# A hybrid attention and RG-LRU block on one core: V's scratch laid out dense by head pair, and the shares' spreads put into the scores' banks

## The chip, the cores and the metric

The kernel runs on one NeuronCore of a Trainium2 chip. The metric is the device time of one execution in microseconds (us), the median of several runs. One further execution is profiled; its own time stands beside its span below. The engines are called PE (TensorE's matmuls), PEld (its weight loads, which run ahead of the matmuls), DVE (VectorE), ACT (ScalarE), POOL (GpSimd) and SP (SyncE, which here only issues transfers).

## The reference, cut to what matters

One decoder block over 2048 positions of width 1024, batch 1, in float32:

```python
proj = x @ W_in + b_in                      # 1024 -> 9216 columns: q, k, v, gates, LRU input
for g, (window, dilation) in enumerate(((128, 1), (512, 4), (2048, 16))):
    # 8 heads of 64; keys t - j*dilation; blocks of 128 queries against 256 keys
    o[g], lse[g] = dilated_band_attention(rope(q[g]), rope(k[g]), v[g], window, dilation)
attn = sum(softmax(lse over g)[g] * o[g])   # the shares of the three groups, per head and position
y_a = (attn * silu(g_attn)) @ w_attn_proj
y_b = (rg_lru(conv(u)) * silu(g_lru)) @ w_lru_proj
out = (sigmoid(gA) * y_a + sigmoid(gB) * y_b) @ w_out + b_out
x = layer_norm(2 ** 0.25 * x + out)
```

A "share" in this text is a softmax weight of a group, one number for each head and position.

## The kernel before

Large products are made of three float32r products each (a tile is split into a high part and a rest, and high by high, high by rest and rest by high are summed in PSUM), which is why almost all matmuls have the form 128x128 by 128x512.

**First stage** (from the start to about 1452 us). The input projection, by a planner: `where` lists 36 pairs of column blocks for each of two halves of the sequence, and `product` (L633) issues 12 matmuls a tick. Results go through chains (generators) that DVE, ACT and POOL serve by a budget per tick. `v_chain` is the one for V: a 128x512 piece of V, channels on the partitions, is turned by four transposes on PE, ACT copies it out of PSUM into one of two tiles `vs` (L374), and SP sends it to the scratch `v_scr` in DRAM (L378). There are 48 such pieces: 3 groups, 4 head pairs, 4 chunks of 512 positions. ACT waits for the transfer that last left a `vs` tile before it fills it again.

**Attention stage** (about 1452 to 1785 us). Its order is written out by hand in the loop `for G in range(NG + 1)`: 48 groups, four of them to a unit, 12 units. A unit is one head pair of one dilation group; it has 16 blocks of 128 queries, and a group takes four of them. On PE a group holds, in this order: `turn_p` of a pair of blocks of the group before (transposes of the probabilities, L1003, into the PSUM banks `t0` and `t1`, one buffer each, copied out by ACT at L1016 and by DVE or ACT for the second half), two `scores` (L975) with another `turn_p` behind them, `values` (L1035, bank `o`, copied out by DVE at L1051), and then twelve matmuls of the other branch's projection (`yb_part`, L1205) in four parts. The scores lie in the banks `s0` and `s1`, two buffers each, one bank for each head of the pair; DVE adds the mask and takes the row minimum (L987), ACT takes the exponential (L989). These eight banks (`s0` and `s1` twice, `t0`, `t1`, `o`, `y`) are all of PSUM.

When the three units of a head pair are done, the shares are worked out (`weights`) and written to DRAM, and come back as `wh`. A **spread** then multiplies them by a selector matrix (L1129, one matmul 128x128 by 128x512), so that each share stands on all 64 partitions of its head, and DVE multiplies the group's output by the bank it lands in (L236, `o<-o,w`). There are 48 spreads: 4 head pairs, 4 chunks, 3 groups. 36 of them run inside the attention loop, up to two in a group, G = 19 to 25, 31 to 37 and 43 to 48: the first between the second and third part of the yb matmuls, the second between the third and fourth. The other 12 run in the next stage out of the bank `z`. Two groups, G = 20 and G = 37, have spreads but no yb matmuls (`rests`), since the next chunk's inputs are then loaded. Every fourth group also ends with a transpose of the minima and sums (`turn_ml`, L1056, bank `o`).

V comes back from `v_scr` unit by unit: `v_parts` issues four transfers of 256 KB for the next unit. At the start of the stage SP issues, one behind the other, V of unit 0, q and k of unit 1, the weights `wlr` and the other branch's inputs `hx` (L1176), V of unit 1 and the second half of `hx`. POOL splits each `hx` into its two parts (L1180, L1181) for the yb matmuls.

**Last stages.** The rest of yb with the last 12 spreads (to about 1873 us), then y_a, the output product and the layer norm. When the attention loop ends, its pool of PSUM is closed and another opened over the same eight banks (`fp`: four buffers of `y`, three of `z`).

Of the kernel before, what the change touches and what calls it, by code (L numbers as in the profile page):

```python
# [8 lines left out]
F32 = mybir.dt.float32  # L9
F32R = mybir.dt.float32r  # L10
AF = mybir.ActivationFunctionType
# [4 lines left out]
P = 128  # L16
S = 2048
# [3 lines left out]
CH = 512  # L21
HP = 4
# [9 lines left out]
def hybrid_block_kernel(ctx: ExitStack, tc: tile.TileContext, a: dict, out: bass.AP):  # L32
    nc = tc.nc
    sp, act, dve, pool, pe = nc.sync, nc.scalar, nc.vector, nc.gpsimd, nc.tensor

    def flat(t):
        return t.bitcast(F32)


    dram = ctx.enter_context(tc.tile_pool(name="dram", bufs=1, space=DRAM))  # L40
# [6 lines left out]
    mg_scr = dram.tile([2 * D, S], F32, name="mg_scr")  # L47
    yb_scr = dram.tile([D, S], F32, name="yb_scr")

    v_scr = [[dram.tile([S, 260], F32, name=f"v_scr{g}{j}") for j in range(2)] for g in range(3)]  # L50

    qk_scr = {(n, u): dram.tile([P, S], F32, name=f"{n}_scr{u}") for u in range(12) for n in ("q", "k")}

# [46 lines left out]
    cur = {}  # L100

    def big(slot, shape, dt, name):
        return (cur["Z"] if slot[0] == "Z" else X).tile(shape, dt, name=name, tag=slot)
# [5 lines left out]
    def later(lag, fn):  # L109
        late.append((now["n"] + lag, fn))  # L110

    def pe_later(lag, fn):
        pe_late.append((now["n"] + lag, fn))

    def run(queue):
        due = [x for x in queue if x[0] <= now["n"]]
        queue[:] = [x for x in queue if x[0] > now["n"]]
        for _, fn in due:
            fn()
# [20 lines left out]
    sl_p = stA.enter_context(tc.tile_pool(name="sl_p", bufs=1))  # L140
# [15 lines left out]
    def give(*ts):  # L156
        for t in ts:
            vacant.append(home.pop(id(t))[0])
# [76 lines left out]
    def tt(eng, out, in0, in1, op):  # L235
        eng.tensor_tensor(out=out, in0=in0, in1=in1, op=op)  # L236
# [113 lines left out]
        give_sent(rp)  # L350


    vs_free = [sl_p.tile([P, 4, 130], F32, name=f"vs{j}") for j in range(2)]
    for t in vs_free:
        dve.memset(t[:, :, 0:1], 1.0)
        dve.memset(t[:, :, 129:130], 1.0)
    tog = {"n": 0}

    def v_chain(vt, sgn, f, c):
        g, hp = divmod(f - FT_V, 4)  # L360
        st = {}

        def turn():
            tp = st["tp"] = ps.tile([P, 4, P], F32, tag="t", name=f"vtp{f}_{c}", bufs=2)
            for b in range(4):
                pe.transpose(tp[:, b, :], flat(vt)[:, b * P:(b + 1) * P], ident)
            give(vt)

        yield Ask(cond=lambda: tog["n"] < 2)
        tog["n"] += 1  # L370
        pe_later(2, turn)
        yield Ask(lag=3, cond=lambda: len(vs_free) > 0, ACT=.66)
        vs = vs_free.pop(0)
        act.activation(vs[:, :, 1:129], st["tp"], AF.Copy, scale=sgn)  # L374
        tog["n"] -= 1
        yield Ask()
        dst = v_scr[g][hp // 2][c * CH:(c + 1) * CH, (hp % 2) * 130:(hp % 2) * 130 + 130]
        sp.dma_start(dst.rearrange("(b p) f -> p b f", p=P), vs)  # L378
        vs_free.append(vs)


# [304 lines left out]
    for s in range(1, NQ):  # L686
        t0 = base[s] - (3 if plan[s][0] else 4)
# [19 lines left out]
    for s, pl in enumerate(plan):  # L707
        if pl[0] and pl[4] == "ug":
            i = pl[1][1][0] - FT_U
# [71 lines left out]
    def unit(u):  # L781

        return (0, 2, 1)[u % 3], u // 3
# [14 lines left out]

    def v_parts(u):
        g, hp = unit(u)  # L800
        src = v_scr[g][hp // 2][:, 130 * (hp % 2) + 1:130 * (hp % 2) + 129]

        def part(i):
            def fn():
                if u == 0 and i == 0:
                    AT_X["v"] = big("X4", [P, 2, 16, P], F32, "V")
                V = AT_X["v"][:, u % 2, 4 * i:4 * i + 4]
                if g == 0:
                    sp.dma_start(V, src[i * CH:(i + 1) * CH].rearrange("(n p) f -> p n f", p=P))
                elif g == 1:  # L810
                    sp.dma_start(V, src[i * CH:(i + 1) * CH].rearrange("(j r) f -> j r f", r=4))
                else:
                    sp.dma_start(V, src.rearrange("(i r) f -> i r f", r=16)[:, 4 * i:4 * i + 4])
            return fn

        return [part(i) for i in range(4)]
# [73 lines left out]
    n = len(where)  # L890
# [32 lines left out]
    def rc(name):  # L923
        return rc_p.tile([P, CH], F32, tag="rc", name=name, bufs=6)

    def gt(name):
        return rc_p.tile([P, CH], F32, tag="gt", name=name, bufs=3)

    def o_tile(u):
        hp, i = divmod(u, 3)  # L930
        x, y = ((2, 0), (2, 1), (1, 1))[i] if hp % 2 == 0 else ((0, 0), (0, 1), (1, 0))[i]
        return OT[x][:, y]
# [21 lines left out]
    st, ML = {}, {}  # L954
# [51 lines left out]
    def copy_p(j, e):  # L1006
        ptb, pt, los = st["t", j]
        on_act = e == 0 or (j % 2 and (j + 1) // 2 in spreads)
        whole = los[0] == los[1]
        for b in (slice(0, 2),) if whole else (slice(0, 1), slice(1, 2)):  # L1010
            lo = los[b.start]
            dst, src = ptb[:, b, :, 64 * e:64 * e + 64], pt[e][:, b]
            if lo:
                dst, src = (t.rearrange("p b (h x) f -> p b h x f", x=2)[:, :, :, 1, :] for t in (dst, src))
            if on_act:
                act.activation(dst, src, AF.Copy)  # L1016
            else:
                dve.tensor_copy(dst, src)
# [105 lines left out]
    def spread(hp, c, g, tag):  # L1124

        cs = slice(c * CH, (c + 1) * CH)
        os = [o_tile(3 * hp + UG[x])[:, cs] for x in range(3)]
        w = cur["ps"].tile([P, CH], F32, tag=tag, name=f"w{hp}{c}{g}", bufs=cur["wb"])
        pe.matmul(w, sel[:, c // 2, g], WH[c % 2], start=True, stop=True)  # L1129
        tt(dve, os[g], os[g], w, ALU.mult)  # L1130
        if g == 0:
            st["ga", hp, c] = rc(f"ga{hp}{c}")
            sp.dma_start(st["ga", hp, c], ga_scr[hp * P:(hp + 1) * P, cs])
            return

        def join():
            tt(pool, os[0], os[0], os[g], ALU.add)
            if g == 1:
                tt(pool, os[0], os[0], st.pop(("ga", hp, c)), ALU.mult)
                if hp == 3 and c == CO[0]:  # L1140
                    later(1, lambda: split(AT[c][:, 3, 0], AT[c][:, 3, 1], os[0]))
                else:
                    pool.dma_start(at_scr[hp * P:(hp + 1) * P, cs], os[0])

        later(1, join)
# [98 lines left out]
            sp.dma_start(ME[c][:, f], yb_scr[f * P:(f + 1) * P, cs])  # L1244
        YG[i] = ga

    cur.update(wb=1, yb=1, ga=lambda i: gt(f"gA{i}"))
    GY = 4
    halves = list(range(64))
    NG = 48  # L1250
# [52 lines left out]
    for hp in range(3):  # L1303
        e = 4 * (3 * hp + 2) + 4
        for i in range(12):
            c, g = i // 3, (0, 2, 1)[i % 3]
# [3 lines left out]
    for G in range(NG + 1):  # L1310
        run(late)
        if G < NG:
            if G:
                turn_p(2 * G - 2)
                copy_p(2 * G - 2, 0)
                copy_p(2 * G - 2, 1)
            scores(2 * G)
            weigh(4 * G)
            weigh(4 * G + 1)
            scores(2 * G + 1)  # L1320
            if G:
                turn_p(2 * G - 1)
                copy_p(2 * G - 1, 0)
                copy_p(2 * G - 1, 1)
            weigh(4 * G + 2)
            weigh(4 * G + 3)
            if G:
                values([j for j in (2 * G - 3, 2 * G - 2) if j >= 0])
        else:
            turn_p(2 * G - 2)  # L1330
            copy_p(2 * G - 2, 0)
            copy_p(2 * G - 2, 1)
            turn_p(2 * G - 1, "s")
            copy_p(2 * G - 1, 0)
            copy_p(2 * G - 1, 1)
            values([2 * G - 3, 2 * G - 2])
            values([2 * G - 1], "s0")
        for fn in todo.pop(G, ()):
            fn()
        y = G >= GY and G not in rests and (G < NG or len(halves) % 2)  # L1340
        if y:
            n, hf = divmod(halves[0], 2)
            yb_part(n, hf, 0)
            yb_part(n, hf, 1)
        two = spreads.pop(G, [])
        if len(two) == 2:
            spread(*two[0], "t1")
        if y:
            yb_part(n, hf, 2)
        if two:  # L1350
            spread(*two[-1], "t0")
        if y:
            yb_part(n, hf, 3)
            if hf:
                yb_done(n)
        if G % 4 == 0 and G:
            turn_ml(G // 4 - 1)
        if y:
            yb_care(halves.pop(0))
            if hf and n in (7, 15):  # L1360
                rests.add(G + 1)
        now["n"] += 1
# [11 lines left out]
    def split(h, l, r, scale=None):  # L1374
        if scale is None:
            act.activation(h, r, AF.Copy)
            dve.tensor_tensor(out=l, in0=r, in1=flat(h), op=ALU.subtract)
        else:
            act.activation(h, r, AF.Copy, scale=scale)
            dve.scalar_tensor_tensor(out=l, in0=r, scalar=scale, in1=flat(h), op0=ALU.mult, op1=ALU.subtract)  # L1380
# [44 lines left out]
    for t in halves:  # L1425
        n, hf = divmod(t, 2)
# [139 lines left out]
    for t, tt in enumerate(TT):  # L1566
        c, b = divmod(t, 4)
# [67 lines left out]
```

## Time and profile before

| what | value |
|---|---|
| median of 3 runs | 2124.18 us (2122.77 to 2124.84) |
| the profiled execution's own time | 2123.79 us |
| its span, first to last instruction | 2122.0 us |
| TensorE clock granted over the span | 0.999 of full speed |
| HBM read and written | 290.00 MB and 151.19 MB |

| stretch | PE busy | DVE busy | ACT busy | POOL busy | DMA engines' busy share |
|---|---|---|---|---|---|
| 0 to 1452 us | 1447.68 | 1173.55 | 926.66 | 458.62 | 0.72 |
| 1452 to 1785 us | 324.32 | 241.00 | 230.88 | 214.51 | 0.85 |
| 1785 to 1873 us | 86.83 | 68.48 | 28.21 | 51.83 | 0.74 |
| 1873 to 2122 us | 240.16 | 177.22 | 31.09 | 39.24 | 0.41 |

A busy PE is not a PE at its peak: a matmul's end is modelled and overlaps the next one's start. In a row of the timeline the columns are the start, the time to the end of the last instruction merged into the row, engine, line, operation, tile written and tiles read, shape and count; in brackets stands how long the engine was idle ahead of it and who released it. In a row of the waits stand the total, the number of waits and the longest, in us.

### The profile page before, as it was taken

The numbers are of one execution on the slowest core, as the hardware profiler recorded it, in microseconds if no ns is written. First come the engines' busy times: TensorE is split into PE (matmuls) and PEld (weight loads), VectorE is DVE, ScalarE is ACT, GpSimd is POOL, SyncE is SP. The second block draws the span as 40 slices with busy tenths as digits, with TensorE's granted clock in tenths as the row PEclk, the third lists the DMA queues.
The fourth block names the chain that finished last, engine by engine and source line by source line (L and its number), as shares of the span: only waits on it lengthen the run. The fifth ranks groups of instructions, "written<-read, shape, count | busy, mean of one in ns | idle before, by whom it ended". The sixth has DMA issues, their size and how long they took to land. (4 is left out here: it accounts for less than half of the span.)

```text
span 2122.0 us, 34703 instructions
## 1 busy us (share of the span) xinstructions
PE 2099.0 (99%) x11637; PEld 1721.6 (81%) x11637; DVE 1660.3 (78%) x2938; ACT 1216.8 (57%) x2502; POOL 764.2 (36%) x692
## 2 busy tenths in 40 slices
PE   9999999999999999999999999999999999999998
PEld 7888888888888888888888888887878788788886
DVE  8787987988989767787677878775777777787667
ACT  6456456467457556677677777676666675321100
POOL 1554654654744301120110111113557678522120
PEclk9999999999999999999999999999999999999999
DMA  7876976976876966676666676769889886774431
GB/s 228 256 222 187 272 225 206 265 224 210 264 230 216 301 189 182 190 206 179 194 199 183 189 229 184 214 194 273 204 214 237 226 229 187 236 240 153 155 99 70
DMA packets 277505, 443.49 MB, mean 209 GB/s; under 512 B 64352, under 2 KB 116608, under 8 KB 274256
## 3 DMA queue, kind: packets, MB, share of 16 engines
q1 hardware_dynamic: 260688, 408.84, 62.8%
q0 software_dynamic: 11744, 23.54, 6.1%
q10 hardware_dynamic: 4896, 8.92, 1.1%
q8 instruction: 92, 1.51, 0.3%
q14 instruction: 85, 0.70, 0.1%
HBM read 290.00 MB, written 151.19 MB: 208 GB/s over the span
## 5 line engine op out<-in xcount | busy, mean ns | idle before, releaser
L633 PE MATMUL q<-xT,hS 128*128 128x512 f32 x1632 | 504.7, 390 | 0.0
L633 PE MATMUL q<-xT,l 128*128 128x512 f32 x1088 | 423.5, 389 | 0.0
L633 PE MATMUL q<-xB,hA 128*128 128x512 f32 x1344 | 417.2, 392 | 0.0
L633 PE MATMUL q<-xB,l 128*128 128x512 f32 x944 | 367.7, 389 | 0.0
L633 PEld LDWEIGHTS q<-xT,hS 128*128 128x128 f32 x1632 | 304.8, 188 | 64.4 <-issue 1.8
L633 PEld LDWEIGHTS q<-xB,hA 128*128 128x128 f32 x1344 | 250.3, 188 | 56.5 <-issue 5.5
L633 PEld LDWEIGHTS q<-xT,l 128*128 128x128 f32 x1088 | 204.3, 188 | 42.5
L236 POOL TENSOR_TENSOR sw<-sw,sin 128x512 f32<-128x512 f32 x96 | 156.1, 1632 | 167.7 <-ACT sw L325 74.0
L633 PEld LDWEIGHTS q<-xB,l 128*128 128x128 f32 x944 | 177.2, 188 | 37.0
L989 ACT ACTIVATE pt<-pt,ml 128x256 f32<-128x256 f32 (+1 forms) x384 | 172.2, 452 | 25.4 <-DVE ml L987 25.4
L236 POOL TENSOR_TENSOR y<-y,h 128x512 f32<-128x512 f32 x28 | 39.1, 1398 | 384.0 <-DVE h L535 368.0
L633 PE MATMUL q<-xB,hS 128*128 128x512 f32 x544 | 168.7, 391 | 1.1 <-DVE v L236 1.1
L633 PE MATMUL q<-xT,hA 128*128 128x512 f32 x544 | 167.9, 390 | 0.0
L280 ACT ACTIVATE hA<-wA 128x512 fp32r<-128x512 f32 x220 | 138.6, 635 | 29.2 <-DVE l L236 11.6
L1205 PE MATMUL yb<-hx,wl 128*128 128x512 f32 x576 | 149.5, 400 | 1.0 <-POOL hx L1181 0.8
L280 ACT ACTIVATE hS<-S 128x512 fp32r<-128x512 f32 x170 | 108.4, 638 | 66.0 <-DVE S L236 47.0
L236 POOL TENSOR_TENSOR l<-wA,hA 128x512 fp32r<-128x512 f32 x68 | 110.1, 1618 | 86.4 <-ACT hA L280 52.5
L1205 PEld LDWEIGHTS yb<-hx,wl 128*128 128x128 f32 x576 | 104.5, 188 | 29.9 <-issue 5.8
L987 DVE CUSTOM_DVE_ANT_0 pt<-s,mask 128x256 f32<-128x256 f32 (+1 forms) x384 | 115.6, 361 | 5.1 <-PE s L975 2.9
L633 PEld LDWEIGHTS q<-xT,hA 128*128 128x128 f32 x544 | 101.8, 188 | 21.7 <-issue 0.4
L633 PEld LDWEIGHTS q<-xB,hS 128*128 128x128 f32 x544 | 101.2, 188 | 22.4 <-issue 1.9
L324 ACT ACTIVATE sw<-y 64x512 f32<-64x512 f32 x96 | 60.6, 631 | 80.6 <-DVE y L577 78.7
(209 smaller groups left out, 4332.1 us busy)
## 6 DMA issues: line engine op xcount, KB each, us to landing
wA<-in_w_in_dram SPq DMA_DIRECT2D x220, 256.0 KB
wl_scr<-l SPq DMA_DIRECT2D x102, 512.0 KB
l<-wl_scr SPq DMA_DIRECT2D x102, 512.0 KB
wS<-in_w_in_dram SPq DMA_DIRECT2D x102, 256.0 KB
wS<-in_w_in_dram POOLq DMA_DIRECT2D x68, 256.0 KB, 6.8
wlr<-in_w_f_dram SPq DMA_DIRECT2D x64, 256.0 KB
mg_scr<-y SPq DMA_DIRECT2D x59, 256.0 KB
v_scr<-vs SPq DMA_DIRECT2D x48, 260.0 KB
```

The costliest lines, as they stand in the source:

```text
L236: eng.tensor_tensor(out=out, in0=in0, in1=in1, op=op)
L280: act.activation(heads(h), heads(r, False), AF.Copy)
L324: act.activation(flat(sw)[lo_], flat(rw)[up_], AF.Copy, scale=scale)
L633: pe.matmul(bank, w[:, ks], x[:, kk, xx], start=(first and i == 0), stop=(last and i == 11))
L987: dve.tensor_tensor_reduce(out=p[:, h, lo:256], in0=bank[h][:, m % 2, lo:256], in1=mask[:, lo:256], scale=1.0, scalar=3e38, op0=ALU.add, o ...
L989: act.activation(p[:, h, lo:256], p[:, h, lo:256], AF.Exp, scale=-1.0, bias=mm, accum_out=ll)
L1205: pe.matmul(YB["t"], w[:, a, k], hx(8 * c + k)[:, b], start=(hf == 0 and m == 0), stop=(hf == 1 and m == 11))
```

## The change

Three edits.

1. **The scratch of V.** `v_scr` was six arrays of 2048 rows by 260 numbers, two head pairs side by side, each pair's 128 channels with a one ahead and a one behind (the ones are read by nobody). It becomes twelve arrays of 2048 by 128, one for each group and head pair. A piece is written without the ones: for the groups of dilation 4 and 16 as 512 runs of 512 bytes (they were 520), for dilation 1 with the rows permuted, so that a partition's four rows lie together, as 128 runs of 2048 bytes. On the way back the four rows that a partition takes lie together for all three groups: a transfer of 256 KB has 128 runs of 2048 bytes where it had 512 of 512.
2. **The tiles `vs`** keep their size (520 numbers a partition), but only the first 512 are used, in one run, and the four memsets that put the ones in are gone.
3. **The spreads** inside the attention loop write to `s0` and `s1` instead of `t1` and `t0`, and take two buffers in turn (`wb=2`). A group with two spreads so moves both `s` rings on by one, and a group with one only that of `s1`.

```diff
-    v_scr = [[dram.tile([S, 260], F32, name=f"v_scr{g}{j}") for j in range(2)] for g in range(3)]
+    v_scr = [[dram.tile([S, P], F32, name=f"v_scr{g}{j}") for j in range(HP)] for g in range(3)]
...
-    vs_free = [sl_p.tile([P, 4, 130], F32, name=f"vs{j}") for j in range(2)]
-    for t in vs_free:
-        dve.memset(t[:, :, 0:1], 1.0)
-        dve.memset(t[:, :, 129:130], 1.0)
+    vs_free = [sl_p.tile([P, 520], F32, name=f"vs{j}")[:, 0:CH].rearrange("p (b f) -> p b f", b=4) for j in range(2)]
...
-        act.activation(vs[:, :, 1:129], st["tp"], AF.Copy, scale=sgn)
+        act.activation(vs, st["tp"], AF.Copy, scale=sgn)
...
-        dst = v_scr[g][hp // 2][c * CH:(c + 1) * CH, (hp % 2) * 130:(hp % 2) * 130 + 130]
-        sp.dma_start(dst.rearrange("(b p) f -> p b f", p=P), vs)
+        if g == 0:
+            sp.dma_start(v_scr[g][hp].rearrange("(p n) f -> p n f", p=P)[:, 4 * c:4 * c + 4], vs)
+        else:
+            sp.dma_start(v_scr[g][hp][c * CH:(c + 1) * CH].rearrange("(b p) f -> p b f", p=P), vs)
...
-        src = v_scr[g][hp // 2][:, 130 * (hp % 2) + 1:130 * (hp % 2) + 129]
+        src = v_scr[g][hp]
...
-                    sp.dma_start(V, src[i * CH:(i + 1) * CH].rearrange("(n p) f -> p n f", p=P))
+                    sp.dma_start(V, src.rearrange("(p n) f -> p n f", p=P)[:, 4 * i:4 * i + 4])
...
-    cur.update(wb=1, yb=1, ga=lambda i: gt(f"gA{i}"))
+    cur.update(wb=2, yb=1, ga=lambda i: gt(f"gA{i}"))
...
-            spread(*two[0], "t1")
+            spread(*two[0], "s0")
...
-            spread(*two[-1], "t0")
+            spread(*two[-1], "s1")
```

No instruction changes its place on any engine; four memsets leave DVE. What moves are the waits. On PE, from the first of two spreads of group 21 on to the scores of group 22, before (a wait is named by the engine, or the transfer's semaphore, that ends it; `w` is the spread, `pt` the transposed probabilities, `s` the scores):

```order
L1129 MATMUL w_16139<-wh_13955,sel 128x512 [waits DMAHW2_49,DMAHW0_49,Activation_49]
L1129 MATMUL w_16147<-wh_13955,sel 128x512
L1003 MATMUL pt_16162<-ident,pt 128x64 [waits DVE_49]
L1003 MATMUL pt_16163<-ident,pt 128x64
...
L975 MATMUL s_16183<-qk_13908 128x256
L975 MATMUL s_16184<-qk_13908 128x256
...
L975 MATMUL s_16197<-qk_13908 128x256
L975 MATMUL s_16198<-qk_13908 128x256
```

and the same rows now:

```order
L1128 MATMUL w_16141<-wh_13957,sel 128x512 [waits DMAHW2_49,DMAHW0_49,DVE_49]
L1128 MATMUL w_16149<-wh_13957,sel 128x512 [waits DVE_49]
L1002 MATMUL pt_16164<-ident,pt 128x64 [waits Activation_49]
L1002 MATMUL pt_16165<-ident,pt 128x64 [waits Activation_49]
...
L974 MATMUL s_16185<-qk_13910 128x256 [waits DVE_49]
L974 MATMUL s_16186<-qk_13910 128x256 [waits DVE_49]
...
L974 MATMUL s_16199<-qk_13910 128x256 [waits DVE_49]
L974 MATMUL s_16200<-qk_13910 128x256 [waits DVE_49]
```

The spread waited for ACT's copy out of the `t` bank, and now for DVE's pass over the scores that lay in its bank; the transposes at the head of the next group waited for DVE's product with the spread, and now only for ACT's copies; and each bank of the next group's scores has a wait for DVE, the second ones for the product with the spread.

The second place is the end of the loop, where the new pool of PSUM opens: the last spreads, the last `turn_ml` and the first yb matmul out of the new pool, on PE, before

```order
L1129 MATMUL w_19099<-wh_13955,sel 128x512 [waits PE_49]
L1129 MATMUL w_19102<-wh_13955,sel 128x512
L1056 MATMUL mlt_19105<-ident,ml_18600 128x128 [waits DVE_49,PE_49]
L1205 MATMUL yb_19122<-hx_13951,wl 128x512 [waits Pool_49]
L1205 MATMUL yb_19122<-hx_13951,wl 128x512 x7
```

and now

```order
L1128 MATMUL w_19101<-wh_13957,sel 128x512 [waits PE_49]
L1128 MATMUL w_19104<-wh_13957,sel 128x512
L1055 MATMUL mlt_19107<-ident,ml_18602 128x128 [waits DVE_49,PE_49]
L1204 MATMUL yb_19124<-hx_13953,wl 128x512 [waits DVE_49,Pool_49]
L1204 MATMUL yb_19124<-hx_13953,wl 128x512 x7
```

The first yb matmul out of the new pool has one wait more, for DVE: its bank is that of `s0` which the last `values` used, and DVE must have copied it out.

## The prediction, made before the changed kernel was run

> **What bounds the kernel now.** I read the page first, then the waits of PE and PEld over the attention stage, and then the timeline at the places that the diff touches. The page:
>
> ```profile
> span 2122.0 us, 34703 instructions
> PE 2099.0 (99%) x11637; PEld 1721.6 (81%) x11637; DVE 1660.3 (78%) x2938; ACT 1216.8 (57%) x2502; POOL 764.2 (36%) x692
> ```
>
> PE is the bound from end to end; all other engines have room. A change that takes no matmul away can only win what PE waits. What PE and PEld waited between 1579 and 1786 us, where the 36 spreads of the loop lie (the first row of PEld's answer, and one of PE's that a rival needs):
>
> ```profile
> PEld pt L1003 <- DVE o L236: 10.9, 19, 1.4
> PE w L1129 <- DMA wh<-w_scr: 1.1, 1, 1.1
> ```
>
> The row that the spreads' edit is about is the first: 19 times the weight load of the next group's transposes waited for DVE's product with a spread. But PEld runs ahead of PE, so its 10.9 us are not all PE's. The boundary of groups 21 and 22, and under it one without a spread:
>
> ```profile
> 1591.68 0.84 PE L1205 MATMUL yb<-hx,wl 128*128 128x512 f32 x3
> 1591.88 0.69 DVE L236 TENSOR_TENSOR o<-o,w 128x512 f32<-128x512 f32 x1 [0.22 <-PE w L1129]
> 1592.62 0.58 PEld L1003 LDWEIGHTS pt<-ident,pt 64*128 64x128 f32 x16 [0.52 <-DVE o L236]
> 1592.62 0.71 PE L1003 MATMUL pt<-ident,pt 64*128 64x64 f32 x16
> ...
> 1536.87 3.01 PE L1205 MATMUL yb<-hx,wl 128*128 128x512 f32 x12
> 1539.81 0.71 PE L1003 MATMUL pt<-ident,pt 64*128 64x64 f32 x16
> ```
>
> With the spread, the transposes start 0.10 us after the last yb matmul's end (1591.68 + 0.84 = 1592.52); without it 0.07 us ahead of that end (1539.88). So of PEld's 0.52 us PE loses 0.17.
>
> **The spreads, part by part.** (a) Thirteen boundaries are like the one above (19 less the two of groups 20 and 37 and four with a `turn_ml`). After the change the transposes need only ACT's copies of `t0` and `t1`, which stand ahead of the spread in the program and are done. 13 x 0.17 = 2.21 us gained. What is late next is the second pair of scores, which goes to the banks that the spreads used: in the row above DVE's product ends at 1592.57; the transposes would start at 1592.45, and the scores behind them take 0.55 us after that (pt to s), their second pair some 0.9 us more. A margin of over a microsecond.
>
> (b) The four boundaries with a `turn_ml` between, with and without a spread:
>
> ```profile
> 1704.15 0.27 PE L1056 MATMUL mlt<-ident,ml 128*128 128x128 f32 x1
> 1704.41 0.45 PEld L1003 LDWEIGHTS pt<-ident,pt 64*128 64x128 f32 x12 [0.34 <-DVE o L236]
> ...
> 1562.36 0.27 PE L1056 MATMUL mlt<-ident,ml 128*128 128x128 f32 x1
> 1562.56 0.47 PE L1003 MATMUL pt<-ident,pt 64*128 64x64 f32 x8
> ```
>
> 0.26 against 0.20 us from start to start: 4 x 0.06 = 0.23 us.
>
> (c) Group 20 has two spreads and no yb matmuls, so nothing lies over the waits:
>
> ```profile
> 1581.74 1.09 PE L1035 MATMUL o<-ptb,V 128*64 128x128 f32 x16
> 1582.88 1.04 DVE L1051 COPY o<-o 128x512 f32<-128x512 f32 x1
> 1583.72 0.74 PE L1129 MATMUL w<-wh,sel 128*128 128x512 f32 x2 [0.89 <-ACT ptb L1016]
> 1584.26 1.28 DVE L236 TENSOR_TENSOR o<-o,w 128x512 f32<-128x512 f32 x2 [0.34 <-PE w L1129]
> 1584.30 0.27 PE L1056 MATMUL mlt<-ident,ml 128*128 128x128 f32 x1
> 1585.60 0.46 PE L1003 MATMUL pt<-ident,pt 64*128 64x64 f32 x8 [1.04 <-DVE o L236]
> ```
>
> Now the spreads go out behind the values, at about 1582.8; `mlt` waits for DVE's copy of the bank `o`, which ends at 1583.92, and starts at about 1584.0; the transposes follow 0.2 us later, at 1584.2 instead of 1585.60. That is 1.40 us. DVE's two products then run from 1583.92 to 1585.2, and the second pair of scores comes to PE at about 1585.4: no wait, but only 0.2 us to spare.
>
> (d) Group 37 has one spread and no yb:
>
> ```profile
> 1708.41 1.05 ACT L1016 ACTIVATE ptb<-pt 128x512 f32<-128x512 f32 x2
> 1710.52 0.71 PE L1003 MATMUL pt<-ident,pt 64*128 64x64 f32 x16 [0.99 <-DVE o L236]
> 1711.33 0.60 ACT L1016 ACTIVATE ptb<-pt 128x512 f32<-128x512 f32 x1
> 1712.86 0.66 PE L1003 MATMUL pt<-ident,pt 64*128 64x64 f32 x16
> ```
>
> The transposes could start when ACT's second copy ends, 1709.46, so 1.0 us sooner; but ACT takes the next copy at 1711.33 whatever PE does, since exponentials stand ahead of it, and the transposes at 1712.86 need its end (1711.93): 0.87 us remain.
>
> (e) Against this stands the new wait at the pool's change:
>
> ```profile
> 1783.91 1.56 DVE L1051 COPY o<-o 128x256 f32<-128x256 f32 x3 [1.63 <-PE o L1035]
> ...
> 1785.26 15.01 PE L1205 MATMUL yb<-hx,wl 128*128 128x512 f32 x65
> ```
>
> DVE's last copy ends at 1785.47, and the first yb matmul started at 1785.26: 0.2 us lost. The waits added to the scores are for events long past; the trace has no row for a satisfied wait. Its bound is 0 to 0.06 us each time (the difference in (b)), for 17 boundaries 0 to 1.0 us; I take 0, because the yb matmuls, which wait for POOL in the program, follow each other without a gap.
>
> **V.** The four memsets are off the path:
>
> ```profile
> L355 DVE MEMSET vs<- x2: 62/62/62, 1.4 to 1.4; 128x4 f32 x2
> ```
>
> They run at 1.4 us, while the first loads are still on their way. ACT's copies keep their count and their 512 numbers. The stores change only what transfers cost; PE has no wait for V's transfers or for ACT in the first stage, so I count nothing there. The way back matters at one place, the start of the attention stage, where the DMA engines are full and SP's transfers queue behind each other:
>
> ```profile
> DMA packets 1202, 0.60 MB, mean 299 GB/s; under 512 B 34, under 2 KB 1202, under 8 KB 1202
> DMA packets 341, 0.59 MB, mean 392 GB/s; under 512 B 38, under 2 KB 59, under 8 KB 341
> 1466.34 0.61 POOL L1180 CAST hx<-hx 128x512 fp32r<-128x512 f32 x1 [11.17 <-DMA hx<-hb_scr]
> 1483.78 0.30 PEld L1205 LDWEIGHTS yb<-hx,wl 128*128 128x128 f32 x2 [0.57 <-POOL hx L1181]
> 1484.34 0.19 PEld L1205 LDWEIGHTS yb<-hx,wl 128*128 128x128 f32 x1 [0.26 <-POOL hx L1180]
> 1485.68 0.30 PEld L1205 LDWEIGHTS yb<-hx,wl 128*128 128x128 f32 x2 [1.16 <-POOL hx L1181]
> ```
>
> The first row is 1449 to 1451 us, nearly all runs of 512 bytes (V of unit 0); the second 1464 to 1465.5 us, nearly all of 2048. V of a unit is 1.05 MB: 3.5 us at 299 GB/s, 2.7 at 392, so `hx` behind it lands 0.8 us sooner, POOL starts its splits 0.8 us sooner, and PE's waits for them (the last three rows: 2.0 us of PEld's, about 1.5 of PE's by the starts of its matmuls) shrink by 0.8. Bounds: 0, if the queue is held elsewhere, and 1.5, all of it. The Trainium skill's page "DMA: Bandwidth & Descriptors" (Specifications) has 512 bytes as the smallest transfer that still runs at line rate; by it 512 and 2048 are alike and this term is 0. The two rows above speak against that: the same engines, 299 and 392 GB/s.
>
> **The sum.** 2.21 + 0.23 + 1.40 + 0.87 + 0.8 - 0.2 = 5.3 us. The profiled execution took 2123.79 us, 0.39 below the median of 2124.18; against its own time that is 2118.5, against the median 2118.9 us. A measurement of this kernel tells about 0.2%, 4.25 us, from no change.
>
> **Rivals.**
> - *Only the spreads pay.* The transfers behind V land no sooner, and the scores' waits cost up to their 1.0 us: 4.5 or less, down to 3.5 us gained, 2119.7 to 2120.7. For it: V is one of several loads in a queue that is full. Against it: the rates above. It is also what the rule of the Trainium skill's page "DMA: Bandwidth & Descriptors" (Specifications) would give.
> - *The gain is swallowed at group 31.* There PE waits for the shares (the 1.1 us row, `wh<-w_scr`). If that transfer kept its time, all that was won ahead of it (0.8 + 1.40 + 5 x 0.17 + 0.06 = 3.1 us) would be waited there: 2.2 us gained, 2122.0. Against it: the chain behind it starts from DVE, which PE paces, so it should move along:
>
> ```profile
> 1639.42 1.43 POOL L236 TENSOR_TENSOR mt<-whl,mt 32x128 f32<-32x128 f32 x3 [10.87 <-DVE whl L236]
> ```
>
> - *The wait moves into the scores.* If DVE ran more than 1 us further behind than in the rows above, PE would wait for the same products one step later: (a) to (d) are gone, 0.6 us stays, 2123.6. Against it: the margin in (a), and that the event is the same one.
> - *More.* The wait for `wh` goes too (1.1 us), all 1.5 us at the start, and PE's waits for DVE in the first stage (1.1, in the row of the next rival): 5.3 + 1.1 + 0.7 + 1.1 = 8.2, 2116.0.
> - *Slower.* DVE is held up at times in the first stage, and that reached PE (a row of the timeline, and PE's only waits for DVE in that stage):
>
> ```profile
> 610.14 5.45 DVE L236 TENSOR_TENSOR l<-wS,hS 128x512 fp32r<-128x512 f32 x1
> ...
> PE q L633 <- DVE v L236: 1.1, 2, 0.8
> ```
>
> One addition took 5.45 us where its like take about 0.7, with POOL at work beside it. Shorter waits of ACT for V's stores shift ACT, DVE and POOL against each other at 48 places; if that made such holds common, each would cost PE up to 0.8 us, and from the seventh on the gain would be gone. Twelve more give 9.6 - 5.3 = 4.3, 2128.5. Against it: there are two such waits in 1452 us. The Trainium skill's page "SBUF — State Buffer" (section "SBUF: two separate sides") has VectorE and GpSimd lock each other out of a shared pair of ports for whole instructions; that fits such a hold, and no run here shows yet what releases it.
>
> **How the numbers follow.** The forecast 0.56, "only the spreads" 0.15, group 31 0.13, the wait moved 0.05, more 0.06, slower 0.05. Forecast and "more" are faster by over 0.2% (below 2119.93): 0.62; the next three lie within 0.2% or, for the first, on its edge: 0.33; slower 0.05. The range reaches from "more" to group 31: 2116.0 to 2122.0; it leaves out the moved wait and the slower case.
>
> **What would show it.** Right: no row "pt from DVE o" of any size; transposes 0.07 us ahead of the last yb's end at every boundary; about 1.4 us less in group 20 and 0.9 in group 37; a first `hx` split of POOL that comes sooner against the stage's start. Wrong: waits of `s` (L974) for DVE, a longer wait of group 31's spread for `wh`, new waits of the first yb matmul beyond 0.2 us at the pool's change, or PE stalls in the first stage.

## The result, and the profile after

The change makes the kernel a little faster: 2119.43 us median (2117.89 to 2123.24, 20 runs) against 2123.27 (2120.48 to 2125.0, 20 runs) of the kernel before on the same chip, a ratio of 0.9982, 95% interval [0.9976, 0.9989]. That is 3.84 us less (2.3 to 5.1 by the interval of the ratio); 5.3 were forecast. Timed once more, with new runs of both kernels, it was 2118.32 against 2123.45, ratio 0.9977 [0.9968, 0.9986], 5.13 us less. The two lie on either side of the 0.2% that the prediction took as its bound. The profiled execution took 2120.95 us, 2.84 less than the profiled one of before. In the changed file the lines stand one lower: the transposes are L1002, the scores L974, the values L1034, the spreads L1128, yb L1204, the copy of the values L1050.

The page, for its first rows:

```profile
span 2119.2 us, 34703 instructions
PE 2098.3 (99%) x11637; PEld 1722.1 (81%) x11637; DVE 1661.1 (78%) x2934; ACT 1217.1 (57%) x2502; POOL 766.0 (36%) x692
```

All that was won is time that PE waited: the matmuls are the same 11637. The waits of PEld and PE between 1579 and 1786 us (engine, line and releaser; us in total, times, the longest):

```profile
PEld pt L1002 <- issue: 8.3, 25, 0.4
PEld pt L1002 <- ACT ptb L1015: 1.4, 2, 1.1
PE pt L1002 <- ACT ptb L1015: 0.9, 1, 0.9
PE mlt L1055 <- DVE o L1050: 0.5, 1, 0.5
```

The row of before with 10.9 us (pt from DVE's o) is gone. What PEld shows instead is "issue", 0.3 us a time, the distance that it keeps to PE at such a boundary anyway. Two rows are new on PE: the transposes waited once for ACT, and `mlt` once for DVE.

The boundary of groups 21 and 22, and under it the end of group 20 up to the scores of group 21, on PE and (its second and third row) DVE:

```profile
1590.59 0.39 PE L1128 MATMUL w<-wh,sel 128*128 128x512 f32 x1
1590.82 0.84 PE L1204 MATMUL yb<-hx,wl 128*128 128x512 f32 x3
1591.59 0.72 PE L1002 MATMUL pt<-ident,pt 64*128 64x64 f32 x16
...
1583.25 0.73 PE L1128 MATMUL w<-wh,sel 128*128 128x512 f32 x2
1583.38 1.04 DVE L1050 COPY o<-o 128x512 f32<-128x512 f32 x1
1584.27 1.25 DVE L236 TENSOR_TENSOR o<-o,w 128x512 f32<-128x512 f32 x2
1584.47 0.33 PE L1055 MATMUL mlt<-ident,ml 128*128 128x128 f32 x1 [0.48 <-DVE o L1050]
1584.73 0.46 PE L1002 MATMUL pt<-ident,pt 64*128 64x64 f32 x8
1585.03 1.73 PE L974 MATMUL s<-qk 64*128 64x256 f32 x14
```

At the boundary the transposes start at 1591.59, 0.07 us ahead of the last yb's end (1590.82 + 0.84 = 1591.66), as without a spread. From the spread's start to theirs it is 1.00 us, where it was 1.17. In group 20 they follow the spreads by 1.48 us (1584.73 - 1583.25) and not by 1.88 (1585.60 - 1583.72 in the row of before), and the spreads no longer wait 0.89 for ACT.

### The profile page after: what moved, and what is told of

It reads as the page before. It is cut to its first block, busy times and chain, and to the rows that moved or that the text cites. A ratio compares the mean times of both kernels' runs of the same rounds, so it can differ in the third digit from the quotient of the medians.

```text
span 2119.2 us, 34703 instructions
## 1 busy us (share of the span) xinstructions
PE 2098.3 (99%) x11637; PEld 1722.1 (81%) x11637; DVE 1661.1 (78%) x2934; ACT 1217.1 (57%) x2502; POOL 766.0 (36%) x692
## 4 chain that ended last, share of the span: by engine, by line
PE 61%; DMA 2%; DVE 1%; POOL 1%; issue 1%; ACT 0%; SPq 0%; DVEq 0%; POOLq 0%
PE q L632 33%; PE yb L1204 7%; PE o L1034 3%; PE s L974 3%; PE z L1511 3%; PE z L1510 3%; PE z L1509 3%; PE pt L1002 2%; PE ya L1477 1%; PE ya L1478 1%; PE ya L1476 1%; PE g L493 1%; DMA V<-v_scr 1%; DMA hx<-hb_scr 1%; PE vtp L363 0%
## 5 line engine op out<-in xcount | busy, mean ns | idle before, releaser
L1204 PE MATMUL yb<-hx,wl 128*128 128x512 f32 x576 | 149.7, 400 | 1.4 <-POOL hx L1180 1.1
L1204 PEld LDWEIGHTS yb<-hx,wl 128*128 128x128 f32 x576 | 104.5, 188 | 30.7 <-issue 6.2
```

What stands on the lines that cost most here:

```text
L1204: pe.matmul(YB["t"], w[:, a, k], hx(8 * c + k)[:, b], start=(hf == 0 and m == 0), stop=(hf == 1 and m == 11))
```

## Where the time went: one table

PE issues the same matmuls in the same order in both kernels, so their starts can be compared one by one. Each column is a stretch between two matmuls, named by when they ran in the profiled execution of before; each number is what the stretch took, in us, less what it took there. "Spreads" are the boundaries at 1590 to 1660, 1668 to 1705 and 1735 to 1783 us together. The rest, with the scatter of the first stage, is in the last column but one.

| kernel | start 1455–1495 | group 20 | spreads | group 31 | group 37 | groups 38–40 | pool change | 1825–1845 | ya 1878–1890 | rest | sum |
|---|---|---|---|---|---|---|---|---|---|---|---|
| before, again | 0.51 | 1.59 | -0.16 | -0.68 | 0.00 | 0.01 | 0.01 | -0.62 | 0.01 | -0.25 | 0.42 |
| after | 0.54 | -1.55 | -2.27 | -1.46 | -1.07 | 1.18 | 0.32 | -0.18 | 1.62 | 0.03 | -2.84 |
| after, again | 0.03 | -1.55 | -2.27 | -0.26 | -1.07 | 0.97 | 0.35 | -0.08 | 0.74 | 0.10 | -3.04 |
| after, third | 0.83 | -1.53 | -2.27 | -0.96 | -1.07 | 0.97 | 0.35 | -1.73 | 0.19 | -2.31 | -7.53 |
| spreads alone | 0.64 | -1.53 | -2.08 | -0.58 | -1.07 | 1.38 | 0.33 | -1.53 | 0.47 | -0.57 | -4.54 |
| V alone | 0.95 | -0.03 | -0.20 | -1.30 | 0.00 | 0.01 | 0.01 | 0.08 | 1.18 | -0.50 | 0.20 |
| after + hx first | -1.62 | -1.56 | -1.74 | -0.82 | -1.07 | 1.57 | 0.32 | -0.71 | 1.23 | -0.57 | -4.97 |
| after + step earlier | -0.32 | -1.52 | -2.26 | -1.11 | -1.07 | 1.22 | 0.33 | -1.37 | 1.50 | 0.06 | -4.54 |
| after + x sooner | 0.23 | -1.52 | -2.25 | -0.75 | -1.07 | 0.94 | 0.32 | -0.64 | -0.67 | 0.54 | -4.87 |
| these three | -1.63 | -1.53 | -2.24 | -1.50 | -1.07 | 1.54 | 0.32 | -0.93 | -0.66 | -0.29 | -7.99 |
| after + exponential later | 0.19 | -1.53 | -2.29 | -1.44 | -1.07 | 0.23 | 0.35 | -0.30 | 1.03 | -0.25 | -5.08 |
| the best | -1.67 | -1.53 | -2.30 | -0.96 | -1.07 | 0.23 | 0.32 | -1.21 | -0.67 | 0.43 | -8.43 |

Two kinds of columns stand in it. Group 20, the spreads, group 37 and the pool's change hardly move among kernels with the spreads moved, and are zero or within 0.2 in those without: they are the change. (The exceptions are a stall of the scores in group 21 of "before, again", and yb's wait for a split of hx by POOL in group 21, which costs about 0.5 us in "hx first" and 0.2 in "spreads alone".) Groups 38 to 40 belong to it too: a loss of 0.9 to 1.6 in every kernel with the spreads moved in which it was not removed, and 0 or 0.01 in the three executions without. Of these columns 0.23 belong to group 37: its transposes come 1.07 sooner, and the next ones, which need ACT's next copy, only 0.83. Group 31, 1825 to 1845 and ya differ between executions of one and the same program by as much as the whole gain of a group; nothing is read from one execution there. What is fixed adds up, for the three executions of the changed kernel, to -3.39, -3.57 and -3.55 us.

## The experiments

**Spreads alone.** The kernel before, with only this:

```diff
-    cur.update(wb=1, yb=1, ga=lambda i: gt(f"gA{i}"))
+    cur.update(wb=2, yb=1, ga=lambda i: gt(f"gA{i}"))
...
-            spread(*two[0], "t1")
+            spread(*two[0], "s0")
...
-            spread(*two[-1], "t0")
+            spread(*two[-1], "s1")
```

> The kernel before with only the spreads moved to the scores' banks (w with two buffers); V as before. Theory (the spreads are the whole gain, V is worth nothing either way): 3.5 to 4.5 us less than before, the same as the full change within 0.6 us; transposes 1.4 us sooner in group 20 and 0.9 in group 37; the 1.09 us wait of group 31's spread for wh is gone here too, because what releases it is not V. Rival (V's dense scratch brings some of it): 2 to 3 us less than before, and the 1.09 us wait for wh still there.

Measured: 2119.95 against 2124.52, 4.57 less, ratio 0.998 [0.9971, 0.9989]. That is the size of the full change. Groups 20 and 37 and, but for 0.2, the boundaries gain what they gain there. Of wh's wait something was left:

```profile
PE w L1129 <- DMA wh<-w_scr: 0.6, 1, 0.6
```

The rival's 2 to 3 us lie below the 4.57, but the interval reaches down to 2.3 less, so the time alone does not rule it out. What speaks against it is that the gains of group 20, the boundaries and group 37 are those of the full change, and that the next run, with V alone, has none of them. The part on wh is answered by the second executions below.

**V alone.** The changed kernel with those same three lines put back.

> The change with the spreads put back into the transposes' banks (w with one buffer), so that only V's dense scratch is left of it. Theory (V is worth nothing): within 0.6 us of before, POOL's first hx split no sooner than in the kernel before (11.2 us idle ahead of it, or up to 0.6 us more), and the 1.09 us wait for wh stays. Rival (V's layout pays as forecast, 0.8 us, and releases wh, 1.1 us): 0.8 to 2 us less than before. Second rival (V's layout costs, by the later hx): 0.5 to 1 us more than before.

Measured: 2122.87 against 2124.52, ratio 0.9996 [0.9987, 1.0004]: no change that can be told from none, but the interval still has room for the 0.8 us that were forecast; what decides is the trace. POOL's first split of `hx` starts at 1466.91 us, in the kernel before at 1466.34: it did not come sooner. Over all executions with the order of loads unaltered, the start's column is 0.35 on average with V dense (seven executions: 0.95, 0.54, 0.03, 0.83, 0.23, -0.32, 0.19) and 0.38 with V as before (three: 0, 0.51, 0.64). The first theory holds at the start. wh's wait was absent in this execution, against it, which the next two runs explain.

**Both kernels again**, for a second profiled execution each, with no edit.

> The changed kernel, unaltered, for a second profiled execution. Theory (the two losses behind the gain belong to the change): the 0.86 us wait of the transposes for ACT's copy in group 40 and 1.5 us or more of waits of ya for the splits of at (L1375 and L1376) are there again, and no wait for wh in group 31. Rival (they are scatter of one execution): one or the other is absent.

> The kernel before, unaltered, for a second profiled execution. Theory: the 1.09 us wait for wh in group 31 is there again, no wait in group 40 and no wait of ya for the splits of at. Rival (scatter): one of the three differs from the first profiled execution.

Measured: 2120.79 and 2124.22, one run each. PE's waits for wh, first in the changed kernel, then in the one before:

```profile
PE w L1128 <- DMA wh<-w_scr: 1.0, 1, 1.0
```

```profile
PE w L1129 <- DMA wh<-w_scr: 0.4, 1, 0.4
```

The wait for wh, missing in the changed kernel's first profile, was there in its second, and in the second of before it was 0.4 in place of 1.1. It is scatter, and "the change released it" would have been a story told from one pair of profiles. Group 40's wait of the transposes for ACT came back (0.6, in the table 0.97 for the stretch); ya's came back smaller (0.74), and V alone had it too (1.18): only partly the change's.

**hx first.** In the changed kernel the queue of SP is reordered at the start of the attention stage:

```diff
-    begin = {1: qk_parts(0), 3: v_parts(0), 5: qk_parts(1)}
+    begin = {1: qk_parts(0), 3: v_parts(0)}
...
     for k in range(4):
         at_group(0, lambda k=k: load_h(k))
-    for fn in v_parts(1):
-        at_group(1, fn)
+    for fn in qk_parts(1):
+        at_group(0, fn)
     for k in range(4, 8):
         at_group(1, lambda k=k: load_h(k))
+    for fn in v_parts(1):
+        at_group(1, fn)
```

> The changed kernel with the loads of hx ahead of the q, k and V of the second unit (q and k of that unit are issued behind the first four hx in group 0, its V behind the last four in group 1). Theory (hx lands late because 2 MB of q and k in runs of 8 KB stand ahead of it, whatever form V has): POOL's first hx split comes 4 us or more sooner, the waits of yb for POOL's hx (1.1 us) go, 1.0 to 1.6 us less than the changed kernel. Rival (hx is held by the release of its buffer or by its source, not by the queue): the first split where it was, no change.

Measured: 2117.11 against 2123.71, 6.60 less, ratio 0.9972 [0.9962, 0.9981]. SP's issues (start, how long SP was at it, what, how many) and POOL's first split, first in the kernel before, then in the changed one, then here:

```profile
1441.85 4.40 SPq L809 DMA_DIRECT2D V<-v_scr  x4
1446.29 3.96 SPq L794 DMA_DIRECT2D qk<-q_scr  x2
1450.29 1.26 SPq L794 DMA_DIRECT2D qk<-k_scr  x2
1452.75 5.70 SPq L1176 DMA_DIRECT2D hx<-hb_scr  x4
```

```profile
1442.04 1.78 SPq L808 DMA_DIRECT2D V<-v_scr  x4
1443.86 1.12 SPq L793 DMA_DIRECT2D qk<-q_scr  x2
1446.91 3.65 SPq L793 DMA_DIRECT2D qk<-k_scr  x2
1453.05 6.42 SPq L1175 DMA_DIRECT2D hx<-hb_scr  x4
1467.06 0.61 POOL L1179 CAST hx<-hx 128x512 fp32r<-128x512 f32 x1 [11.69 <-DMA hx<-hb_scr]
```

```profile
1446.94 4.28 SPq L1175 DMA_DIRECT2D hx<-hb_scr  x4
1451.57 1.13 SPq L793 DMA_DIRECT2D qk<-q_scr  x2
1455.27 0.61 POOL L1179 CAST hx<-hx 128x512 fp32r<-128x512 f32 x1 [0.56 <-DMA hx<-hb_scr]
```

The dense V took SP 2.6 us less to issue, but V itself was through no sooner (shown below, under V), and 2 MB of q and k (four transfers of 512 KB) stand between V and hx. Behind q and k 1.0 us of the 2.6 was left (k's issue ends at 1450.56, against 1451.55 in before), and when hx began, nothing (1453.05 against 1452.75). With hx ahead of q and k the first split comes 11.8 us sooner and the start's column falls to -1.62. The theory holds, with more gain than it expected: about 2 us against the mean of the changed kernel's three executions (0.47), and the column is the same in both other kernels that have this edit (-1.63, -1.67).

**Step earlier.**

```diff
-        for i, g in enumerate((1, 3, 3, 4)):
+        for i, g in enumerate((1, 2, 3, 4)):
```

> The changed kernel with the first step of each head pair's shares (the minimum of the three sums, DVE and POOL) one group earlier, the rest where it was. Theory (in group 40 ACT's exponential waits for POOL's subtractions and holds up ACT's copy behind it, 0.86 us of PE): that wait is gone, 0.6 to 1.0 us less than the changed kernel if nothing later takes it, and 0 where the wait of ya for its loads takes it back. Rival (the copy is late for another reason, DVE's 1.38 us operation beside POOL): the wait stays.

Measured: 2118.19 against 2123.71, 5.52 less, ratio 0.9978 [0.9969, 0.9986]: inside the scatter of the changed kernel. The wait for ACT in group 40 is gone, as the theory had it, but another came in group 39. DVE, then PE:

```profile
1713.66 0.82 DVE L236 TENSOR_TENSOR whl<-mt 32x128 f32<-32x128 f32 x1 [2.38 <-DMA mt<-ml_scr]
1714.51 1.35 DVE L236 TENSOR_TENSOR whl<-whl,mt 32x128 f32<-32x128 f32 x1
1715.79 0.67 DVE L1017 COPY ptb<-pt 128x512 f32<-128x512 f32 x1
...
1716.52 0.71 PE L1002 MATMUL pt<-ident,pt 64*128 64x64 f32 x15 [0.72 <-DVE ptb L1017]
```

One group earlier, the step's sums have not landed, DVE stands 2.38 us for them, and its copy of the transposes behind it is late. The loss of groups 38 to 40 stays at 1.22. I moved the wait, not the cause.

**x sooner.** In the last stage the changed kernel loads the first x tile and the first vector at job 4:

```diff
+        if i == 4:
+            load_xr(TT[0])
+            load_vec(0)
         if i == 7:
-            load_xr(TT[0])
-            load_vec(0)
             parts = bring_at(1)
```

> The changed kernel with the loads of the first x tile and the first vector (1 MB) three jobs earlier in the last stage, ahead of the four at loads instead of just before them. Theory (the DMA engines are full from 8 us ahead of the second ya group, so PE, which comes 4.5 us sooner, waits for the loads there and gives 1.6 us back): the waits of ya for the splits of at (0.5 and 1.2 us) go, 1.2 to 1.8 us less than the changed kernel. Rival (they wait for ACT or DVE, not for the loads): no change.

Measured: 2117.54 against 2123.71, 6.17 less, ratio 0.9973 [0.9964, 0.9982]. Of the longest pieces of the changed kernel's chain of waits the last in time is a transfer that y_a needs, issued behind the x tile and the vector:

```profile
1872.53 8.15 DMA atr<-at_scr
```

ACT's splits of what it brings, in the changed kernel and then in this one:

```profile
1879.44 2.54 ACT L1375 ACTIVATE at<-atr 128x512 fp32r<-128x512 f32 x4 [1.68 <-PE z L1510]
```

```profile
1875.83 2.70 ACT L1375 ACTIVATE at<-atr 128x512 fp32r<-128x512 f32 x4 [0.17 <-DMA atr<-at_scr]
```

The splits come 3.6 us sooner, and ya's column is -0.67 here and within 0.01 of that in both other kernels that have this edit: the kernel before had lost 0.67 there too. The theory holds: 1.5 us less than the mean of the changed kernel's three executions (0.85). It is the columns that say so, here and for "hx first": the intervals of both times overlap that of the changed kernel, which was not timed beside them.

**These three together.**

> The three edits together on the changed kernel: hx loads first, the shares' first step one group earlier, the first x tile and vector earlier. Theory: the gains add up, 1.0 to 1.6, 0.6 to 1.0 and 1.2 to 1.8 us: 2.8 to 4.4 us less than the changed kernel, about 7 to 8 less than before. Rival (each gain is taken back by the next wait that stands at a transfer): under 2 us less than the changed kernel.

Measured: 2115.47 against 2123.71, 8.24 less, ratio 0.9966 [0.9954, 0.9978]; beside the changed kernel's 3.84 and 5.13 that is 3.1 to 4.4 more, about the sum of the first and third edit by their columns (2.1 and 1.5), so these two gains add up, though the second edit gave none of it (1.54 in its column).

**Exponential later.** The step that holds ACT up is put behind the copies it stood ahead of, and nothing is made earlier:

```diff
-        for i, g in enumerate((1, 3, 3, 4)):
+        for i, g in ((0, 1), (1, 3), (3, 4)):
             at_group(e + g, lambda hp=hp, i=i: step(hp, i))
+        mid[e + 4] = lambda hp=hp: step(hp, 2)
...
                 copy_p(2 * G - 2, 1)
+            mid.pop(G, lambda: None)()
             scores(2 * G)
```

> The changed kernel with the sums' step of the shares (ACT's exponential and POOL's products behind it) put behind the first two copies of the group that follows, so that the exponential no longer stands ahead of ACT's copy in groups 16, 28 and 40; the step before it stays where it was. Theory (the gain of group 37 is handed back in group 40, because POOL is full there and ACT's copy queues behind an exponential that waits for POOL): the wait of 0.6 to 0.9 us in group 40 is gone and nothing takes its place before the last stage, PE 0.9 to 1.3 us further ahead at 1780 us; of that 0 to 1.3 us reaches the end, since the loads at ya can take it. Rival (POOL's lag comes out at another place, as it did when the step before was moved, where DVE waited for its load): a new wait of 0.7 us or more between groups 38 and 44.

Measured: 2118.27 against 2123.45, 5.18 less, ratio 0.9975 [0.9964, 0.9985], beside 5.13 of the changed kernel on the same chip. Groups 38 to 40 now lose 0.23 and not 0.97 or 1.18. These 0.23 are group 37's, as said under the table: behind them nothing is lost, where the changed kernel lost 0.73 to 0.95 in group 40. No wait took the place between groups 38 and 44; but the time is the same. In the profiled execution PE's largest wait behind that is at ya, in the loads that "x sooner" is about:

```profile
PE ya L1479 <- DVE at L1378: 1.2, 1, 1.2
```

So the mechanism in group 40 is confirmed; that the 0.7 to 0.95 us are lost again at ya is likely, but ya waits in other executions as well, and the times alone do not tell it.

**The best**: hx first, x sooner, exponential later.

> The changed kernel with hx loaded first, the first x tile and vector three jobs sooner, and the sums' step behind the copies. Theory: the three gains add up, 1.0 to 1.6, 1.2 to 1.8 and 0.9 to 1.3 us: 3.1 to 4.7 us less than the changed kernel, and about 1 us less than the kernel with the three edits before, where the third only moved its wait. Rival: no less than that kernel (8.2 us less than before).

Measured: 2114.54 against 2123.45, 8.91 less, ratio 0.9955 [0.9941, 0.9969], the fastest here and 3.8 us less than the changed kernel on the same chip. Its distance to the kernel with the three edits above (0.9966 [0.9954, 0.9978]) is within the intervals; by the table the exponential's place is worth 1.3 there (0.23 against 1.54).

**The changed kernel, timed beside these.**

> The changed kernel, unaltered, timed beside these. Both theories: 3.5 to 5 us less than before; a third profiled execution shows the wait of group 40 and the waits of ya again, and a wait for wh of anything from 0 to 1.1 us.

Measured: the second pair of times at the head of this text, 5.13 less. Group 40's wait and ya's came again, each 0.6. Its profiled execution took 2116.28 us, 4.7 less than the first one of the same program: 2.3 in the first stage, 1.5 at 1825 to 1845 and 1.4 at ya, and 0.8 the other way at the start and in group 31.

## Why the prediction was right, and where not

The sign, the cause and nearly the size were right: PE waited at the spreads' boundaries for DVE, and those waits went. Step by step:

- **(a) and (b), the boundaries**: 2.44 forecast. From the start of the last spread to that of the next transposes, eleven boundaries of the three stretches took 1.17 us before and 1.00 after, the four with a `turn_ml` 1.17 and 1.11, each to within 0.01; one more lies in the column of group 20, and one, less exact, in that of group 31. So the forecast is right. Of the 2.27 in the table 2.1 are these; the other 0.16 show without the spreads moved too (-0.16 and -0.20). The margin of over a microsecond ahead of the scores held: no wait of s for DVE shows.
- **(c), group 20**: 1.40 forecast; 1.53 to 1.55 less the first boundary's 0.17, 1.36 to 1.38. Right.
- **(d), group 37**: 1.0 forecast at its transposes and 0.87 to remain behind ACT's next copy; 1.07 and 0.83 were measured. So far it was right, but it stopped at that copy, and in group 40 PE handed back 0.73 to 0.95, about as much as had remained. This step failed. What was late there was POOL:

```profile
1696.00:1721.00 25.00, 25.00 (x295) 20.97 (x290) 19.77 (x70) 19.10 (x69) 23.45 (x26) 1.00 0.84 222
```

In these 25 us of the changed kernel (columns: length; busy us of PE, PEld, DVE, ACT and POOL with their counts; granted clock, DMA share, GB/s) POOL is busy 23.45; it was as full in the kernel before (24.81 of the 26.40 us from 1698 on). It splits hx and weights and joins the shares, and what was gained in group 37 did not reach it: from the kernel before to the changed one PE's transposes below came 4.56 us sooner (1726.06 to 1721.50), ACT's exponential behind POOL's products 3.59 (1726.56 to 1722.97). In group 39 the step of the shares then goes DVE, POOL, ACT, and ACT's copy for group 40 stands behind it. The chain in the changed kernel, and under it the end of the same chain in the kernel before:

```profile
1719.86 1.33 POOL L236 TENSOR_TENSOR wl<-wlr,wl 128x512 fp32r<-128x512 f32 x1
1720.06 1.38 DVE L236 TENSOR_TENSOR whl<-whl,mt 32x128 f32<-32x128 f32 x1
1721.50 0.71 PE L1002 MATMUL pt<-ident,pt 64*128 64x64 f32 x16
1721.52 1.42 POOL L236 TENSOR_TENSOR mt<-whl,mt 32x128 f32<-32x128 f32 x3 [0.33 <-DVE whl L236]
1722.97 0.52 ACT L1101 ACTIVATE mt<-mt 32x384 f32<-32x384 f32 x1 [2.58 <-POOL mt L236]
1723.40 0.57 ACT L1015 ACTIVATE ptb<-pt 128x512 f32<-128x512 f32 x1
1724.02 0.71 PE L1002 MATMUL pt<-ident,pt 64*128 64x64 f32 x16 [0.86 <-ACT ptb L1015]
```

```profile
1724.63 0.39 DVE L236 TENSOR_TENSOR whl<-whl,mt 32x128 f32<-32x128 f32 x1
1726.06 0.71 PE L1003 MATMUL pt<-ident,pt 64*128 64x64 f32 x16
1726.56 0.52 ACT L1102 ACTIVATE mt<-mt 32x384 f32<-32x384 f32 x1 [1.61 <-POOL mt L236]
1726.99 0.57 ACT L1016 ACTIVATE ptb<-pt 128x512 f32<-128x512 f32 x1
```

Before, the copy started 0.93 us after its transposes, and PE did not wait; now 1.90 after them. That this queue is the cause was shown by moving the exponential behind the copies. DVE's instruction of 1.38 us, 0.39 before, is at most 0.33 us of the lag, for so long POOL idled ahead of its own step. In "spreads alone" it took 0.70, POOL did not idle there at all, and PE still waited 1.1 us ("hx first": 0.71 and 1.3):

```profile
1720.49 0.70 DVE L236 TENSOR_TENSOR whl<-whl,mt 32x128 f32<-32x128 f32 x1
1722.31 1.41 POOL L236 TENSOR_TENSOR mt<-whl,mt 32x128 f32<-32x128 f32 x3
PE pt L1003 <- ACT ptb L1016: 1.1, 1, 1.1
```
- **(e), the pool's change**: 0.2 forecast, 0.32 to 0.35 measured. DVE's last copies and the first yb in the changed kernel:

```profile
1779.42 1.56 DVE L1050 COPY o<-o 128x256 f32<-128x256 f32 x3 [1.63 <-PE o L1034]
1781.13 3.19 PE L1204 MATMUL yb<-hx,wl 128*128 128x512 f32 x13
```

The yb starts 0.15 us after the copy's end (1780.98), which the sum had left out. No cost shows for the satisfied waits.
- **V**: 0.8 forecast, nothing measured. The step that failed comes ahead of "hx behind it lands 0.8 us sooner": V itself was through no sooner. Its packets ran from 1447.9 to 1452.5 us in the kernel before and from 1448.0 to 1453.2 in the changed one. The DMA engines in the 5 us from 1448 on, in which nearly all of them lie, before and then changed:

```profile
DMA packets 2238, 1.65 MB, mean 330 GB/s; under 512 B 86, under 2 KB 2126, under 8 KB 2202
DMA packets 689, 1.60 MB, mean 319 GB/s; under 512 B 92, under 2 KB 92, under 8 KB 641
```

In runs of 2 KB the engines moved no more bytes here. The forecast had put the 392 GB/s of a later stretch, of other loads, into this one. Why the rate did not come with the longer runs stays open; q and k, in runs of 8 KB, are loaded beside V. For V of unit 1 it does show (305 GB/s from 1466 to 1469 us before, 380 now), but no gain of PE followed. What held hx besides was the 2 MB of q and k ahead of it. That is the rival "only the spreads pay", in its main point.
- **Group 31**: the gain was not swallowed there. Its wait for wh differs from 0 to 1.1 us between executions.
- **Slower**: the first stage took as long as before (0.2 us apart in the two first profiles), and the 5.45 us addition stands at its old place in it.

The sum with the steps as measured: 5.3, less V's 0.8, less 0.8 in group 40 (the mean of three), less 0.14 at the pool's change, is about 3.6, against 3.4 to 3.6 in the fixed columns. The medians, 3.84 and 5.13 (4.57 with the spreads alone), lie above it by 0.3 to 1.6. What fills that is open: the columns that scatter can hold it, and neither three executions of one kernel nor two of the other settle their means.

## What to carry to other kernels

When a wait goes, follow every engine that feeds the next groups, not only the one that ends the next wait: an engine that is 94% busy in that stretch, as POOL here, may not come sooner with PE, and the gain is handed back where its result is next in someone's queue. A rate read in one stretch need not hold in another where other loads share the engines: V in longer runs was issued 2.6 us faster and was through no sooner. Reordering the queue was worth 2 us where the longer runs were worth none. Compare the starts of the same instructions over two executions of each kernel before a wait that came or went is called an effect of the change.

## What the runs showed of the hardware

- One program's executions differ by place: 4.7 us between two profiles of the changed kernel, in two stalls of the first stage (625 and 705 us) and at the places of the table that scatter, at a granted clock of 0.999 in both.
- A small DVE instruction with both inputs in SBUF, beside a POOL instruction that had begun first, is held to that one's end. The 32x128 operation of 0.39 us took 1.38 with POOL's addition from 1719.86 to 1721.19 beside it, ending at 1721.44. In "step earlier" it took 1.35, ending at 1715.86, and this is what POOL ran (1714.33 + 1.30 = 1715.63):

```profile
1714.33 1.30 POOL L236 TENSOR_TENSOR o<-o,ga 128x512 f32<-128x512 f32 x1
```

Both end some 0.24 us after POOL's; in "spreads alone" the same operation, 0.70 us long, ends as far behind a shorter POOL instruction. The Trainium skill's page "SBUF — State Buffer" (section "SBUF: two separate sides") has the two engines share a pair of ports that whoever starts first keeps for the whole instruction, for a DVE instruction with two inputs in SBUF against a POOL instruction that reads SBUF; these rows agree. An instruction of 0.4 us can so take a microsecond longer. In the chain of group 40 that cost POOL only 0.33 us.
